# Rotary embedding on one core: four VectorE operations per batch instead of ten, and the tables in float32 on the SyncE queue

## The chip, the cores and the metric

The kernel runs on one core of one Trainium2 chip. The metric is the time of one execution in microseconds (us); medians of several runs are given, with their range. A profile gives the *span*, from the first to the last instruction of the core; here a run's time is 1.7 to 2.2 us longer than its span.

The core has several engines that work at the same time. VectorE (DVE in the profile) does all the arithmetic here, ScalarE (ACT) the small casts and the negation of the changed kernel, GpSimd (POOL) only issues transfers and SyncE (SP) issues the table transfers of the changed kernel. Sixteen DMA engines move the bytes. In the packet records (below) a transfer of a batch is 128 packets, and they start in rounds of 16; I read this as eight packets for each engine, worked off in order.

## The reference

```python
def setup_inputs():
    batch, seq_len, num_heads, head_dim = (8, 2048, 16, 64)
    return {'x': np.random.randn(batch, seq_len, num_heads, head_dim).astype(np.float32),
            'cos': np.random.randn(seq_len, head_dim // 2).astype(np.float32),
            'sin': np.random.randn(seq_len, head_dim // 2).astype(np.float32)}

def reference(x, cos, sin):
    head_dim = x.shape[-1]
    x1 = x[..., :head_dim // 2]
    x2 = x[..., head_dim // 2:]
    cos = cos[None, :, None, :]
    sin = sin[None, :, None, :]
    out1 = x1 * cos - x2 * sin
    out2 = x1 * sin + x2 * cos
    return np.concatenate([out1, out2], axis=-1).astype(np.float32)
```

The input x and the output are 8 batches of 8.39 MB each in float32 (2048 x 16 x 64 x 4 bytes). Each table has 0.26 MB.

## The kernel before

A batch is one tile of 128 partitions with 16384 float16 values each. GpSimd's queue casts from float32 on the way in and back on the way out. Five tiles can be in use. VectorE works in place, on half a batch at a time.

```python
    const_pool = ctx.enter_context(tc.tile_pool(name="rope_const", bufs=1))
    io_pool = ctx.enter_context(tc.tile_pool(name="rope_io", bufs=5))
    tmp_pool = ctx.enter_context(tc.tile_pool(name="rope_tmp", bufs=2))
    # ... load(b): one transfer on nc.gpsimd, x[b] -> a [P, J, H, D] float16 tile
    def tables():
        nc.gpsimd.dma_start(out=sin_sb, in_=sin.rearrange("(p j) d -> p (j d)", j=J))
        nc.gpsimd.dma_start(out=cos_sb, in_=cos.rearrange("(p j) d -> p (j d)", j=J))

    def rotate(xt):
        for j0 in range(0, J, JC):          # J = 16, JC = 8: two halves
            # ... v1, v2: temporaries; x1, x2: halves of the head; sin_b, cos_b: broadcasts
            nc.vector.tensor_mul(out=v1, in0=x2, in1=sin_b)      # L55
            nc.vector.tensor_mul(out=v2, in0=x1, in1=sin_b)      # L56
            nc.vector.tensor_mul(out=xw, in0=xw, in1=cos_b)      # L58
            nc.vector.tensor_sub(out=x1, in0=x1, in1=v1)         # L59
            nc.vector.tensor_add(out=x2, in0=x2, in1=v2)         # L60

    for b in range(B):
        tiles[b] = load(b)                                       # L37
        if b == 0:
            tables()                                             # L43, L44
        if b >= 4:
            nc.gpsimd.dma_start(out=out[b - 4]..., in_=tiles[b - 4])   # L68
        rotate(tiles[b])
    # ... the stores of the last four batches                     L73
```

The scheduler may reorder the instructions of one queue where the data allow it. In what follows L0 to L7 are the loads of the batches and S0 to S7 their stores.

## Time and profile before

| | before |
|---|---|
| time, median of 3 (range) | 318.91 us (318.77 to 319.09) |
| span of the profiled run | 317.2 us |
| HBM bytes | 67.63 MB read, 67.11 MB written |
| VectorE busy | 210.7 us, 66% |
| first VectorE operation | 24.26 us |
| last store issued | 265.27 us |

From the page of the kernel before: busy time, the span in 40 slices (a digit is the busy share of a slice in tenths), the DMA queue and the HBM bytes.

```profile
DVE 210.7 (66%) x80; POOL 9.9 (3%) x22
...
DVE  0009999999999999999069999995009994000000
...
DMA  7979999999999999999999999999999999999996
...
q0 software_dynamic: 2592, 100.93, 99.6%
...
HBM read 67.63 MB, written 67.11 MB: 425 GB/s over the span
```

The DMA row is the one to look at: 9 nearly from end to end. VectorE has holes. The transfers move 134.7 MB in 317.2 us, and while the row stays like this only fewer bytes or a higher rate would shorten them. The 425 GB/s is what the Trainium skill gives for a core that streams alone ("HBM Reference", Specifications (TRN2)), and near the 435 GB/s that it names as the fabric's ceiling ("DMA: Bandwidth & Descriptors", Specifications). The page puts that ceiling at the ports of the on-chip memory, where here only the float16 bytes pass, half as many.

Two of the groups of instructions (busy us, mean ns of one; then the idle time before them and what ended most of it), and the view of waits (us in total, times, longest):

```profile
L55 DVE TENSOR_TENSOR v<-xt,sin_sb 128x4096 f16<-128x4096 f16 x16 | 36.5, 2284 | 54.2 <-DMA xt<-in_x_dram 29.9
L58 DVE TENSOR_TENSOR xt<-xt,cos_sb 128x8192 f16<-128x8192 f16 x16 | 70.7, 4416 | 0.0
```

```profile
POOL xt L37 <- DMA out_dram<-xt: 118.1, 3, 56.4
...
DVE v L55 <- DMA xt<-in_x_dram: 29.9, 2, 20.2
DVE v L55 <- DMA sin_sb<-in_sin_dram: 24.3, 1, 24.3
```

GpSimd waits 118 us for stores to land before it may load a tile again. Whether that hurts is told by the order of its issues. The timeline of the kernel before (start, duration, what; in brackets the idle time before and what ended it):

```profile
2.96 2.14 POOL L37 DMA_DIRECT2D xt<-in_x_dram  x4
24.26 2.29 DVE L55 TENSOR_TENSOR v<-xt,sin_sb 128x4096 f16<-128x4096 f16 x1 [24.26 <-DMA sin_sb<-in_sin_dram]
...
53.13 0.54 POOL L68 DMA_DIRECT2D out_dram<-xt  x1 [48.03 <-DVE xt L60]
...
79.41 0.54 POOL L68 DMA_DIRECT2D out_dram<-xt  x1 [25.74 <-DVE xt L60]
...
123.00 0.54 POOL L37 DMA_DIRECT2D xt<-in_x_dram  x1 [43.05 <-DMA out_dram<-xt]
...
142.13 0.53 POOL L37 DMA_DIRECT2D xt<-in_x_dram  x1 [18.60 <-DMA out_dram<-xt]
...
142.66 1.06 POOL L68 DMA_DIRECT2D out_dram<-xt  x2
...
200.15 0.54 POOL L37 DMA_DIRECT2D xt<-in_x_dram  x1 [56.42 <-DMA out_dram<-xt]
200.67 1.05 POOL L73 DMA_DIRECT2D out_dram<-xt  x2
...
265.27 0.53 POOL L73 DMA_DIRECT2D out_dram<-xt  x1 [46.18 <-DVE xt L60]
```

Read as letters this is L0 to L4, S0 S1, L5 L6, S2 S3, L7, S4 S5 S6 S7. When L5 waits for S0 to land, S1 is already queued behind it; when L6 waits for S1, L5 is. So the engines never run dry, and GpSimd's waits cost nothing.

### The profile page before, as it was taken

To read this page: it belongs to the slowest core of one execution; us is meant where nothing else is said; L and a number is where in the kernel's file an instruction comes from. 1 tells how busy PE (TensorE), PEld (TensorE's weight loads), DVE (VectorE), ACT (ScalarE), POOL (GpSimd) and SP (SyncE) were. 2 spreads that over 40 slices of the span, in tenths; PEclk is the share of its full clock that TensorE was granted. 3 is DMA by queue.
4 is the path that set the end of the run, shared out by engine and by line. 5 is a ranking of instruction groups with operands and counts; after the bars stand their busy time and mean duration, and the time that the engine had idled before them with its cause. 6 is when DMAs were issued, how large, how long until landed. Compare 5 with 4: busy or idle time off the path is not lost.

```text
span 317.2 us, 164 instructions
## 1 busy us (share of the span) xinstructions
DVE 210.7 (66%) x80; POOL 9.9 (3%) x22
## 2 busy tenths in 40 slices
DVE  0009999999999999999069999995009994000000
POOL 5000000000000000001000000100000000000000
DMA  7979999999999999999999999999999999999996
GB/s 132 256 163 266 207 198 202 260 198 198 198 264 264 397 397 529 397 331 231 231 198 199 380 413 397 454 471 264 198 314 413 397 446 479 397 397 512 413 397 264
DMA packets 2593, 100.93 MB, mean 318 GB/s; under 512 B 288, under 2 KB 544, under 8 KB 544
## 3 DMA queue, kind: packets, MB, share of 16 engines
q0 software_dynamic: 2592, 100.93, 99.6%
q14 instruction: 1, 0.01, 0.0%
HBM read 67.63 MB, written 67.11 MB: 425 GB/s over the span
## 4 chain that ended last, share of the span: by engine, by line
issue 34%; DMA 19%; DVE 16%; another core or an unknown queue 13%; POOL 1%; POOLq 0%; DVEq 0%; PEldq 0%
DMA xt<-in_x_dram 12%; DMA sin_sb<-in_sin_dram 7%; DVE xt L58 5%; DVE v L55 3%; DVE xt L60 3%; DVE v L56 3%; DVE xt L59 2%; POOL xt L37 1%; POOL out_dram L68 1%; POOLq L101 0%; POOLq L37 0%; POOLq L73 0%; DVEq L55 0%; PEldq L101 0%
## 5 line engine op out<-in xcount | busy, mean ns | idle before, releaser
L55 DVE TENSOR_TENSOR v<-xt,sin_sb 128x4096 f16<-128x4096 f16 x16 | 36.5, 2284 | 54.2 <-DMA xt<-in_x_dram 29.9
L58 DVE TENSOR_TENSOR xt<-xt,cos_sb 128x8192 f16<-128x8192 f16 x16 | 70.7, 4416 | 0.0
L59 DVE TENSOR_TENSOR xt<-xt,v 128x4096 f16<-128x4096 f16 x16 | 36.5, 2283 | 0.1
L60 DVE TENSOR_TENSOR xt<-xt,v 128x4096 f16<-128x4096 f16 x16 | 36.5, 2283 | 0.0
L56 DVE TENSOR_TENSOR v<-xt,sin_sb 128x4096 f16<-128x4096 f16 x16 | 36.5, 2283 | 0.0
L37 POOL DMA_DIRECT2D xt<-in_x_dram x8 | 4.4, 568 | 118.9 <-DMA out_dram<-xt 118.1
L68 POOL DMA_DIRECT2D out_dram<-xt x4 | 2.1, 539 | 73.8 <-DVE xt L60 73.8
L73 POOL DMA_DIRECT2D out_dram<-xt x4 | 2.1, 532 | 63.0 <-DVE xt L60 63.0
L44 POOL DMA_DIRECT2D cos_sb<-in_cos_dram x1 | 0.5, 548 | 0.0
L43 POOL DMA_DIRECT2D sin_sb<-in_sin_dram x1 | 0.5, 542 | 0.0
L90 POOL MEMSET const-float32-0.0<- 128x1 f32 x1 | 0.1, 100 | 0.2 <-issue 0.2
L90 POOL MEMSET const-bfloat16-1.0<- 128x1 bf16 x1 | 0.1, 103 | 0.0
L90 POOL MEMSET const-float32-1.0<- 128x1 f32 x1 | 0.1, 100 | 0.0
L90 POOL MEMSET const-uint8-127<- 128x1 uint8 x1 | 0.1, 100 | 0.0
## 6 DMA issues: line engine op xcount, KB each, us to landing
xt<-in_x_dram POOLq DMA_DIRECT2D x8, 4096.0 KB, 39.8
sin_sb<-in_sin_dram POOLq DMA_DIRECT2D x1, 128.0 KB, 22.2
cos_sb<-in_cos_dram POOLq DMA_DIRECT2D x1, 128.0 KB, 22.4
out_dram<-xt POOLq DMA_DIRECT2D x8, 65.9
```

The source lines that it names most:

```text
L37: nc.gpsimd.dma_start(out=xt, in_=x[b].rearrange("(p j) h d -> p (j h d)", j=J))
L43: nc.gpsimd.dma_start(out=sin_sb, in_=sin.rearrange("(p j) d -> p (j d)", j=J))
L44: nc.gpsimd.dma_start(out=cos_sb, in_=cos.rearrange("(p j) d -> p (j d)", j=J))
L55: nc.vector.tensor_mul(out=v1, in0=x2, in1=sin_b)
L56: nc.vector.tensor_mul(out=v2, in0=x1, in1=sin_b)
L58: nc.vector.tensor_mul(out=xw, in0=xw, in1=cos_b)
L59: nc.vector.tensor_sub(out=x1, in0=x1, in1=v1)
L60: nc.vector.tensor_add(out=x2, in0=x2, in1=v2)
L68: nc.gpsimd.dma_start(out=out[b - 4].rearrange("(p j) h d -> p (j h d)", j=J), in_=tiles[b - 4])
L73: nc.gpsimd.dma_start(out=out[b].rearrange("(p j) h d -> p (j h d)", j=J), in_=tiles[b])
L90: nc = _bacc.Bacc("TRN2", target_bir_lowering=False, num_devices=1)
```

## The change

The intent is fewer, longer VectorE operations, a subtract turned into an add by a negated sine table, and tables that no longer stand in the software queue.

```diff
-    JC = 8
+    NBUF = 5
-    tmp_pool = ctx.enter_context(tc.tile_pool(name="rope_tmp", bufs=2))
+    tmp_pool = ctx.enter_context(tc.tile_pool(name="rope_tmp", bufs=1))
-    cos_sb = const_pool.tile([P, J, Dh], f16)
-    sin_sb = const_pool.tile([P, J, Dh], f16)
+    # sin_f, cos_f: float32 tiles; cos_h, sin_h, neg_h: float16 tiles
+    nc.sync.dma_start(out=sin_f, in_=sin.rearrange("(p j) d -> p j d", j=J))
+    nc.sync.dma_start(out=cos_f, in_=cos.rearrange("(p j) d -> p j d", j=J))
     # ... load unchanged; the tables() of before is gone
     def rotate(xt):
-        for j0 in range(0, J, JC):
-            # ... the five operations of a half
+        v = tmp_pool.tile([P, J, H, D], f16)
+        # ... sin_b, neg_b, cos_b: broadcasts over the heads
+        nc.vector.tensor_mul(out=v[:, :, :, 0:Dh], in0=xt[:, :, :, Dh:D], in1=neg_b)   # L58
+        nc.vector.tensor_mul(out=v[:, :, :, Dh:D], in0=xt[:, :, :, 0:Dh], in1=sin_b)   # L59
+        xw = xt.rearrange("p j h (e d) -> p j (h e) d", d=Dh)
+        nc.vector.tensor_mul(out=xw, in0=xw, in1=cos_b)                                # L61
+        xa = xt.rearrange("p j h d -> p (j h d)")
+        nc.vector.tensor_add(out=xa, in0=xa, in1=v.rearrange("p j h d -> p (j h d)"))  # L63
+    tiles = [load(b) for b in range(NBUF)]
+    nc.scalar.copy(out=sin_h, in_=sin_f)
+    nc.scalar.mul(out=neg_h, in_=sin_f, mul=-1.0)
+    nc.scalar.copy(out=cos_h, in_=cos_f)
     for b in range(B):
-        # ... load, store of b - 4, rotate
+        rotate(tiles[b])
+        store(b, tiles[b])                       # the same transfer, now L49
+        if b + NBUF < B:
+            tiles.append(load(b + NBUF))         # L43
```

More of the change, by code (lines that the diff above doesn't have):

```diff
@@ L20 @@
     f16 = mybir.dt.float16
+    f32 = mybir.dt.float32
     B, S, H, D = x.shape
@@ L25 @@
     J = S // P
-    JC = 8
+    NBUF = 5
     const_pool = ctx.enter_context(tc.tile_pool(name="rope_const", bufs=1))
-    io_pool = ctx.enter_context(tc.tile_pool(name="rope_io", bufs=5))
-    tmp_pool = ctx.enter_context(tc.tile_pool(name="rope_tmp", bufs=2))
-    cos_sb = const_pool.tile([P, J, Dh], f16)
-    sin_sb = const_pool.tile([P, J, Dh], f16)
+    io_pool = ctx.enter_context(tc.tile_pool(name="rope_io", bufs=NBUF))
+    tmp_pool = ctx.enter_context(tc.tile_pool(name="rope_tmp", bufs=1))
+    sin_f = const_pool.tile([P, J, Dh], f32)
+    cos_f = const_pool.tile([P, J, Dh], f32)
+    cos_h = const_pool.tile([P, J, Dh], f16)
+    sin_h = const_pool.tile([P, J, Dh], f16)
+    neg_h = const_pool.tile([P, J, Dh], f16)
+    nc.sync.dma_start(out=sin_f, in_=sin.rearrange("(p j) d -> p j d", j=J))
+    nc.sync.dma_start(out=cos_f, in_=cos.rearrange("(p j) d -> p j d", j=J))
     def load(b):
@@ L40, in load, with store @@
         return xt
-    def tables():
-        nc.gpsimd.dma_start(out=sin_sb, in_=sin.rearrange("(p j) d -> p (j d)", j=J))
-        nc.gpsimd.dma_start(out=cos_sb, in_=cos.rearrange("(p j) d -> p (j d)", j=J))
+    def store(b, xt):
+        nc.gpsimd.dma_start(
+            out=out[b].rearrange("(p j) h d -> p (j h d)", j=J), in_=xt
+        )
     def rotate(xt):
-        for j0 in range(0, J, JC):
-            js = slice(j0, j0 + JC)
-            v1 = tmp_pool.tile([P, JC, H, Dh], f16)
-            v2 = tmp_pool.tile([P, JC, H, Dh], f16)
-            x1 = xt[:, js, :, 0:Dh]
-            x2 = xt[:, js, :, Dh:D]
-            sin_b = sin_sb[:, js, :].unsqueeze(2).to_broadcast([P, JC, H, Dh])
-            cos_b = cos_sb[:, js, :].unsqueeze(2).to_broadcast([P, JC, 2 * H, Dh])
-            nc.vector.tensor_mul(out=v1, in0=x2, in1=sin_b)
-            nc.vector.tensor_mul(out=v2, in0=x1, in1=sin_b)
-            xw = xt[:, js, :, :].rearrange("p j h (e d) -> p j (h e) d", d=Dh)
-            nc.vector.tensor_mul(out=xw, in0=xw, in1=cos_b)
-            nc.vector.tensor_sub(out=x1, in0=x1, in1=v1)
-            nc.vector.tensor_add(out=x2, in0=x2, in1=v2)
@@ L62 @@
-    tiles = {}
-    for b in range(B):
-        tiles[b] = load(b)
-        if b == 0:
-            tables()
-        if b >= 4:
-            nc.gpsimd.dma_start(
-                out=out[b - 4].rearrange("(p j) h d -> p (j h d)", j=J), in_=tiles[b - 4]
-            )
+        v = tmp_pool.tile([P, J, H, D], f16)
+        sin_b = sin_h.unsqueeze(2).to_broadcast([P, J, H, Dh])
+        neg_b = neg_h.unsqueeze(2).to_broadcast([P, J, H, Dh])
+        cos_b = cos_h.unsqueeze(2).to_broadcast([P, J, 2 * H, Dh])
@@ L71 @@
+    nc.scalar.mul(out=neg_h, in_=sin_f, mul=-1.0)
+    nc.scalar.copy(out=cos_h, in_=cos_f)
+    for b in range(B):
         rotate(tiles[b])
-    for b in range(B - 4, B):
-        nc.gpsimd.dma_start(
-            out=out[b].rearrange("(p j) h d -> p (j h d)", j=J), in_=tiles[b]
-        )
+        store(b, tiles[b])
+        if b + NBUF < B:
+            tiles.append(load(b + NBUF))
 _INS = ['x', 'cos', 'sin']
```

## The prediction

> **What bounds the kernel now.** The transfers. In the slice table the DMA row is at 9 tenths nearly throughout; the queue table gives 99.6% of the 16 engines' span to one software queue. The kernel reads 67.63 MB and writes 67.11 MB of HBM, 425 GB/s over the 317.2 us span: 16 big transfers (8 loads, 8 stores) of 8.4 MB of float32, about 315/16 = 19.7 us each. The table by windows agrees: the load-only stretch 26 to 98 us moves 216 to 221 GB/s counted in float16, so 432 to 442 in float32; two stores back to back (98 to 142 us) move 405. VectorE is busy 210.7 us (66%), behind the transfers; it waits 29.9 us for loads of x and 24.3 us for the first data (view of waits). GpSimd's waits (118.1 us for stores to land before a buffer is loaded again) cost nothing: in the timeline other transfers are queued during each.
>
> **What the change does.** VectorE: a batch takes 8 operations of 4096 columns (start to start 2.20 us) and 2 of 8192 (4.34 us): 26.3 us. Afterwards two of 8192 and two of 16384: the same elements. The durations 2283 and 4416 ns give 0.52 ns an element, the two elements a cycle that the Trainium skill ("VectorE: DVE Perf Modes", Side-by-side) gives tensor_tensor at best; bigger operations gain no mode. Estimate: 2 x 4.34 + 2 x 8.6 = 25.9 us a batch; busy time falls from 210.7 to about 208 us, none of it critical.
>
> Tables: the first VectorE operation waited until 24.2 us for the sine table, queued behind the first load. It should start near 22 us, when the load lands. Nothing is gained at the end: the same bytes go through the same 16 engines, as the Trainium skill says ("DMA: Bandwidth & Descriptors", Issuing engines are not separate DMA queues).
>
> **Critical path.** Bytes of x and out: unchanged. Gain 0 to 1 us.
>
> **The risk: order on GpSimd's queue.** Before, the issues came as five loads, S0 S1 L5 L6 S2 S3 L7 S4 to S7 (S store, L load), so a transfer was always queued while a load waited for a store. The diff can't show the scheduled order. If it becomes S0 L5 S1 L6 S2 L7, each of the three loads waits with an empty queue. One such gap, estimated from the trace's end (312 to 317.2 us at a 0.48 share: 2.7 us lost) and start (1.9 us before any bytes), costs 3 to 4 us, so 9 to 12 us. Chance: about one in four.
>
> **Prediction.** 318.5 us; 316 to 327 holds it 8 times in 10. Faster by over 2%: 0.03. Within 2%: 0.75. Slower by over 2%: 0.22.
>
> **What would show each step right or wrong.** VectorE's groups: 8192 near 4.4 us, 16384 near 8.7 us, busy 206 to 209 us. First VectorE operation at 21 to 23 us, released by the load of x, not a table. DMA at 9 tenths in all slices; HBM bytes 0.3 MB more at most. A DMA slice at 8 or less in the middle, just after a load's wait for a store, would show the bad order.
>
> **What would make it wrong.** That order; loads and stores mixed on the engines at another rate than 405 to 440 GB/s; operations of 16384 columns at a different rate; a last load landing so late that VectorE's 26 us for it empties the queue before the last store.

## The result, and the profile after

The changed kernel took 318.04 us (median of 6, 317.98 to 318.18) and the kernel before 319.03 us (median of 6, 318.77 to 319.15) on the same chip. The difference is 1.0 us in the medians and 0.9 us in the spans of the profiled runs (316.3 against 317.2). The ratio is 0.997, with a 95% interval of 0.9957 to 0.9983. A ratio is the mean time of one kernel's fast runs over that of the other's fast runs of the same rounds, so it is not quite the ratio of the medians. Whether even this 0.3% is a property of the kernel is taken up below: on another chip it was not there.

From the page of the changed kernel, the same lines as of the kernel before:

```profile
DVE 209.2 (66%) x32; ACT 2.9 (1%) x4; POOL 8.8 (3%) x20
...
DVE  0009999999999999999579999990009993000000
...
DMA  8999999999999999999999999999999999999996
...
q0 software_dynamic: 2304, 100.66, 99.4%
q1 hardware_dynamic: 288, 0.52, 0.4%
...
HBM read 67.63 MB, written 67.11 MB: 426 GB/s over the span
```

VectorE went from 80 instructions to 32 and from 210.7 to 209.2 us. The DMA row is what it was, except for two slices: the first, where the tables arrive on queue q1, rose from 7 to 8 tenths, and the third from 7 to 9, because there L1 now follows L0 at once where the tables had stood between them. The groups and the waits:

```profile
L58 DVE TENSOR_TENSOR v<-xt,neg_h 128x8192 f16<-128x8192 f16 x8 | 35.4, 4426 | 54.1 <-DMA xt<-in_x_dram 53.9
L61 DVE TENSOR_TENSOR xt<-xt,cos_h 128x16384 f16<-128x16384 f16 x8 | 69.5, 8692 | 0.3
```

```profile
POOL xt L43 <- DMA out_dram<-xt: 120.2, 3, 56.4
DVE v L58 <- DMA xt<-in_x_dram: 53.9, 3, 24.8
```

An operation of 16384 columns takes 8.69 us and one of 8192 takes 4.42 us; before, one of 8192 took 4.42 us as well. VectorE's waits for data stay at 54 us: 29.9 for loads and 24.3 for the sine table before, 53.9 for loads now. The timeline of the changed kernel shows the same order of transfers:

```profile
1.25 2.79 POOL L43 DMA_DIRECT2D xt<-in_x_dram  x5 [0.80 <-PEq L99]
...
23.60 4.43 DVE L58 TENSOR_TENSOR v<-xt,neg_h 128x8192 f16<-128x8192 f16 x1 [23.60 <-DMA xt<-in_x_dram]
...
50.18 0.54 POOL L49 DMA_DIRECT2D out_dram<-xt  x1 [46.15 <-DVE xt L63]
...
76.43 0.54 POOL L49 DMA_DIRECT2D out_dram<-xt  x1 [25.70 <-DVE xt L63]
...
121.98 0.53 POOL L43 DMA_DIRECT2D xt<-in_x_dram  x1 [45.02 <-DMA out_dram<-xt]
...
141.29 0.53 POOL L43 DMA_DIRECT2D xt<-in_x_dram  x1 [18.78 <-DMA out_dram<-xt]
141.81 1.06 POOL L49 DMA_DIRECT2D out_dram<-xt  x2
...
199.26 0.53 POOL L43 DMA_DIRECT2D xt<-in_x_dram  x1 [56.38 <-DMA out_dram<-xt]
199.78 1.05 POOL L49 DMA_DIRECT2D out_dram<-xt  x2
...
264.13 0.53 POOL L49 DMA_DIRECT2D out_dram<-xt  x1 [50.50 <-DVE xt L63]
```

S0 goes out 3 us earlier than before (50.18 against 53.13), and S1 likewise (76.43 against 79.41), because VectorE starts 0.7 us earlier and no longer weaves two batches into each other. But L5, which waits for S0 to *land*, starts only 1 us earlier (121.98 against 123.00): S0 stands in line behind L0 to L4, and the line moves at the engines' pace.

### The profile page after: what moved, and what is told of

Same layout as the page of the kernel before. It is cut to its first block, busy times and chain, and to the rows that moved or that the text cites. A ratio compares the mean times of both kernels' runs of the same rounds, so it can differ in the third digit from the quotient of the medians.

```text
span 316.3 us, 121 instructions
## 1 busy us (share of the span) xinstructions
DVE 209.2 (66%) x32; ACT 2.9 (1%) x4; POOL 8.8 (3%) x20
## 4 chain that ended last, share of the span: by engine, by line
issue 33%; DMA 19%; DVE 17%; another core or an unknown queue 14%; POOL 1%; POOLq 0%; DVEq 0%; PEldq 0%
DMA xt<-in_x_dram 19%; DVE xt L63 6%; DVE xt L61 6%; DVE v L58 3%; DVE v L59 3%; POOL out_dram L49 1%; POOL xt L43 0%; POOLq L99 0%; POOLq L49 0%; DVEq L61 0%; DVEq L58 0%; PEldq L99 0%
## 5 line engine op out<-in xcount | busy, mean ns | idle before, releaser
L58 DVE TENSOR_TENSOR v<-xt,neg_h 128x8192 f16<-128x8192 f16 x8 | 35.4, 4426 | 54.1 <-DMA xt<-in_x_dram 53.9
L61 DVE TENSOR_TENSOR xt<-xt,cos_h 128x16384 f16<-128x16384 f16 x8 | 69.5, 8692 | 0.3
L63 DVE TENSOR_TENSOR xt<-xt,v 128x16384 f16<-128x16384 f16 x8 | 69.5, 8692 | 0.3
L59 DVE TENSOR_TENSOR v<-xt,sin_h 128x8192 f16<-128x8192 f16 x8 | 35.3, 4418 | 0.0
```

The costliest lines, as they stand in the source:

```text
L58: nc.vector.tensor_mul(out=v[:, :, :, 0:Dh], in0=xt[:, :, :, Dh:D], in1=neg_b)
L59: nc.vector.tensor_mul(out=v[:, :, :, Dh:D], in0=xt[:, :, :, 0:Dh], in1=sin_b)
L63: nc.vector.tensor_add(out=xa, in0=xa, in1=v.rearrange("p j h d -> p (j h d)"))
```

## The experiments

Eleven kernels ran. The trace also holds a record of each packet that a DMA engine moved. A load packet of x fills one partition: 65,536 bytes of float32 read, 32,768 of float16 written. A store packet is the reverse. The quickest load packets took 2.431 us and the store packets 2.447 us on average; so an engine needs 8 packets, about 19.3 us from one transfer's start to the next one's, for its share of a batch either way. (8.39 MB in 19.33 us is 434 GB/s.)

### Is VectorE anywhere in the chain? Less of it, and more of it

The first edit leaves one operation per batch of the four. The result is wrong.

```diff
-        nc.vector.tensor_mul(out=v[:, :, :, 0:Dh], ...)
-        nc.vector.tensor_mul(out=v[:, :, :, Dh:D], ...)
         nc.vector.tensor_mul(out=xw, in0=xw, in1=cos_b)
-        nc.vector.tensor_add(out=xa, ...)
```

> The changed kernel with one VectorE operation per batch (the cosine product of 16384 columns) instead of four, wrong on purpose. Theory D (the transfers alone set the time): VectorE busy falls from 209 to about 70 us and the time stays at 318.0 us within 0.3. Rival (VectorE's time sits in the chain, through the first operations or the last store): a fall of the order of the 17.4 us that one batch loses, to about 300 us.

It took 318.29 us (median of 4, 317.71 to 318.80; ratio to the kernel before 0.9978). From its page:

```profile
DVE 69.5 (22%) x8; ACT 3.0 (1%) x4; POOL 8.8 (3%) x20
...
DVE  0009155090550900000073280000009100000000
...
DMA  8999999999999999999999999999999999999996
```

VectorE lost 140 of its 209 us and the time did not follow. The rival falls.

The second edit adds a fifth operation, whose result is overwritten. The output stays right.

```diff
+        nc.vector.tensor_mul(out=v.rearrange("p j h d -> p (j h d)"), in0=x0, in1=x0)
         nc.vector.tensor_mul(out=v[:, :, :, 0:Dh], in0=xt[:, :, :, Dh:D], in1=neg_b)
```

> The changed kernel with a fifth VectorE operation of 16384 columns per batch, whose result is overwritten, so the output stays right. VectorE needs 8 x 8.7 = 70 us more. Theory D with a limit: VectorE hides until the last store goes out later than the engines run dry, near 295 us; with 34.9 us a batch from 23.6 us on it goes out near 303 us, so the time is 326 to 329 us, about 10 us more and not 70. Rival D2 (VectorE hides at any length up to the span): 318.0 us. Rival V (VectorE is on the chain throughout): 388 us.

It took 328.64 us (median of 4, 328.05 to 330.38; ratio 1.0312), as expected of VectorE with a limit. Its page, a line of its timeline and a stretch of its table by windows (start to end, length, VectorE, ScalarE and GpSimd busy, PE clock, DMA share, GB/s):

```profile
DVE 278.7 (85%) x40; ACT 2.9 (1%) x4; POOL 8.8 (3%) x20
...
DMA  8989989989989999989989999998899999990896
```

```profile
303.89 0.53 POOL L49 DMA_DIRECT2D out_dram<-xt  x1 [34.44 <-DVE xt L65]
```

```profile
295.00:304.00 9.00, 8.60 (x1) 0.00 (x0) 0.10 (x1) 1.00 0.00 0
```

The 0 near the end of the DMA row is the limit: VectorE finished the last batch at 303.6 us, and in the window from 295 to 304 us no packet begins. In the changed kernel the last store is issued at 264.1 us, and its first packet starts at 294.7 us by the packet records. VectorE thus has some 30 us of slack. Of the 70 us more work another 30 went into its own waits for loads (53.9 us in the changed kernel; here the view of waits has the line below), and only about 10 came out as time. What the change saves on VectorE (1.5 us of busy time) only makes this slack longer.

```profile
DVE v L59 <- DMA xt<-in_x_dram: 23.7, 1, 23.7
```

### Which half of the change moved the 0.3%?

One kernel has the tables alone, the other the operations alone.

```diff
 # tables alone: the kernel before, with
-        nc.gpsimd.dma_start(out=sin_sb, ...)     # and cos_sb, software queue
+    nc.sync.dma_start(out=sin_f, ...)            # and cos_f, float32, SyncE queue
+        nc.scalar.copy(out=sin_sb, in_=sin_f)    # and cos_sb
```

```diff
 # operations alone: the changed kernel, with
-    nc.sync.dma_start(out=sin_f, ...)            # and cos_f
+        nc.gpsimd.dma_start(out=sin_h, ...)      # and cos_h, after load(0)
+        nc.scalar.mul(out=neg_h, in_=sin_h, mul=-1.0)
```

> The kernel before with only the tables changed: float32 on the SyncE queue, cast by two ScalarE copies; its ten VectorE operations per batch stay. Theory T (the 0.9 us that the change gained are the tables leaving the software queue and filling the idle start): about 318.0 us, as the changed kernel, with the last packet ending 0.9 us earlier than before. Rival V (the gain comes from the four longer VectorE operations, each store going out a little earlier): 319.0 us, as before.

> The changed kernel with only its VectorE side: four operations per batch and a negated table, but the tables come as float16 on the software queue behind the first load, as before. Theory T: 319.0 us, as before. Rival V: 318.0 us.

The operations alone took 318.80 us (median of 5, 318.64 to 319.12; ratio 0.9996): as before, so nothing of the 0.3% shows on the VectorE side. The tables alone took 318.54 us (median of 6) but spread from 317.91 to 320.35 us; its ratio, 0.9996 with an interval of 0.9976 to 1.0016, decides nothing. So both it and the changed kernel ran again, side by side on another chip.

> The tables-alone kernel once more, unchanged, because its timed runs spread from 317.9 to 320.4 us and settled nothing. Theory T: median 318.0 to 318.5 us, and equal to the changed kernel run beside it. Rival V: 319.0 us, 0.9 us above the changed kernel run beside it.

> The changed kernel, unchanged, beside the two others on one chip. If its 0.9 us gain is real, its median lies 0.5 to 1.2 us under the kernel before; if not, it is within 0.3 us of it.

The tables alone took 318.94 us (median of 6, 318.54 to 320.68; ratio 1.0011). The changed kernel took 319.61 us (median of 6, 317.88 to 320.08; ratio 1.0012, interval 0.9993 to 1.0031), beside 318.98 us for the kernel before. By its own expectation the gain of 0.9 us is not confirmed; a median 0.6 us above the kernel before lies outside both outcomes. The tables alone fit neither as a whole: 318.9 us is rival V's number, but 0.7 us under the changed kernel beside it and not 0.9 above. What is there is a wider spread: with the tables on SyncE's queue runs at this speed lie between 317.7 and 320.7 us, while the kernel before stays within 318.6 to 319.3 us on every chip, the operations alone within 318.6 to 319.1 and the kernel without tables (below) within 317.3 to 317.9.

The packet records of the profiled runs show where the spread comes from. The columns: when the first and the last of the 16 engines begin with x, when they begin with S0, when the last two of them end, and the mean of all 16 ends. (The records do not name the engine; the 16 earliest packets are taken for the 16 engines' first ones, and a late engine is followed by its lateness.)

| profiled run (us) | span | begin x, first / last | begin S0, first / last | last two ends | mean end |
|---|---|---|---|---|---|
| before | 317.2 | 2.61 / 3.83 | 102.27 / 102.75 | 315.24, 315.41 | 314.98 |
| operations alone | 317.4 | 2.63 / 3.45 | 102.31 / 103.01 | 315.31, 315.50 | 315.05 |
| changed | 316.3 | 3.42 / 3.82 | 101.56 / 102.01 | 314.39, 314.50 | 314.22 |
| changed, again | 318.3 | 3.44 / 5.30 | 101.37 / 103.76 | 314.32, 316.55 | 314.26 |
| tables alone | 316.3 | 3.50 / 3.86 | 101.40 / 101.78 | 314.26, 314.59 | 314.11 |
| tables alone, again | 317.2 | 3.24 / 4.62 | 101.14 / 103.02 | 315.42, 315.50 | 314.37 |

In the profile of the repeated run the changed kernel has one engine that begins with x at 5.30 us, 1.5 us after the second latest of 3.80, and the last end stands 2.2 us after the second last. The other fifteen end by 314.32 us, 1.1 us before the last one of the kernel before. A spread at the start can shrink during the loads (in the kernel before from 1.2 us to 0.5 us by S0), but from S0 on lateness is not made up (in the repeated run the last engine is 1.9 us behind the next at S0 and 2.2 us at the end), and the slowest engine sets the time. So in all four profiles with the tables on SyncE's queue the engines end 0.6 to 0.9 us earlier on average than in the two without, the repeated ones included; and in two of the four late engines give that back or more. That the late start comes from the table packets is likely, since it was seen only with them (also in the profile of the forced order below, with two engines at 5.29 and 5.55 us), but it is not proven. On the first chip none of the changed kernel's six runs shows it, on the other most seem to; whether the chip decides, and which engine it is, stays open.

### Are the tables free on their own queue?

The tables are left out; constants stand in, and the result is wrong.

```diff
-    nc.sync.dma_start(out=sin_f, ...)            # and cos_f
-    nc.scalar.copy(out=sin_h, in_=sin_f)         # and neg_h, cos_h
+    nc.vector.memset(sin_h, 0.5)                 # and neg_h, cos_h
```

> The changed kernel with no tables loaded at all; constants are written in their place, so the result is wrong on purpose. Theory T1 (in the changed kernel the tables still cost engine time: they hold back the first packet of x from 2.6 to 3.4 us): the first packet of x starts at 2.6 us and the time is 317.2 us, 0.8 less than the changed kernel. Rival T2 (on the hardware queue the tables are free, all hidden before x starts): 318.0 us, as the changed kernel.

It took 317.58 us (median of 5, 317.31 to 317.87; ratio 0.9958), between the two expectations. The packet records decide. The first packet of x starts at 2.61 us, as T1 said. The start of L1 alone would mislead: with all engines starting at once from idle, the first round of 16 packets took 3.15 us on average instead of 2.43, and L1 began at 22.6 us. In the changed kernel x begins 0.8 us later, at 3.42 us, its first round took only 2.49 us, and L1 began at 22.8 us. In the kernel before, with 1.56 us of table packets per engine between L0 and L1 (256 packets of 98 ns over 16 engines) and a slow first round of 3.12 us, L1 began at 24.0 us. By that mark the tables on SyncE's queue would cost 0.2 us. But the four loads that follow even the slow first round out: averaged over the 16 engines, x begins at 2.87 us without tables and at 3.56 us in the changed kernel, S0 at 101.03 and 101.73 us, and the last packet ends at 313.52 and 314.22 us, 0.7 us apart each time. In the kernel before S0 begins at 102.45 us and the mean end is 314.98 us. The tables thus cost some 1.4 us on the software queue and 0.7 us on SyncE's in these profiles, late engines aside: theory T1, with 0.7 where it said 0.8. They cost less on SyncE's queue because their first packet starts at 2.01 us, 0.6 us before x could begin, and so fills idle time: 256 packets of 87 ns are 1.4 us for each engine, of which some 0.8 us are left.

The one-operation run above also shows what happens when a table packet comes too late. In its records four table packets, which I take to be one engine's, stand alone at 6.25, 8.75, 11.26 and 13.76 us, 2.5 us apart: one for each packet of x. This is what the Trainium skill says of the queues of one engine ("DMA: Bandwidth & Descriptors", Queues, rings and completion order): it takes turns between them, a whole packet at a time. A 2,048-byte table packet beside 65,536-byte packets waits for a whole one of them each time.

### The order that the prediction feared

Each store is tied, in issue order only, behind the transfer that precedes it in the source.

```diff
     def store(b, xt):
+        with tc.issue_after(queued[-1].ins):
             queued.append(nc.gpsimd.dma_start(out=out[b]..., in_=xt))
```

> The changed kernel with its transfers forced into the order in which the source writes them: five loads, S0 L5 S1 L6 S2 L7 S3 to S7. Theory Q (my prediction's risk: loads 5, 6 and 7 each wait for a store with nothing else queued): three gaps in the DMA row near 120, 160 and 200 us of 3 to 4 us each, so 327 to 330 us. Rival (the engines do not all finish together, the fast ones work on while the slow ones end, and the gap is smaller or hidden): 318 to 322 us.

It took 332.34 us (median of 4, 331.07 to 333.62; ratio 1.0422), 13 us more, and a little over the range that I had given. Its DMA row and queue share, and its timeline:

```profile
DMA  7989899898998939989889989789999989899995
...
q0 software_dynamic: 2304, 100.66, 96.5%
```

```profile
124.25 0.53 POOL L45 DMA_DIRECT2D xt<-in_x_dram  x1 [71.11 <-DMA out_dram<-xt]
124.77 0.54 POOL L52 DMA_DIRECT2D out_dram<-xt  x1
167.32 0.53 POOL L45 DMA_DIRECT2D xt<-in_x_dram  x1 [42.02 <-DMA out_dram<-xt]
167.85 0.54 POOL L52 DMA_DIRECT2D out_dram<-xt  x1
210.53 0.53 POOL L45 DMA_DIRECT2D xt<-in_x_dram  x1 [42.15 <-DMA out_dram<-xt]
```

L5 waits for S0 with nothing behind S0. By the packet records the engines stand idle for 4.55, 2.44 and 2.45 us on average at the three places: 9.4 us, within the 9 to 12 that the prediction estimated. The first gap is the longer because two engines, late from the start, end S0 2.2 us after the others; from the last end to the first new packet it is 1.9 us at all three places. The rest is in the packets. Of L5, L6 and L7 the first round took 3.06, 3.00 and 3.21 us and the last round, before the store, 3.78, 3.90 and 3.60 us, against 2.43 in between: about 2 us for each load, 6.0 us in all. Together 15.4 us, of the 15.6 us between the spans (331.8 and 316.3 us). The profiled run is the slowest of the four (333.62 us). With three gaps of 2.4 us and 6.0 us of slow packets, an estimate without late engines gives 13.3 us, near the 13.4 us between the medians. The first five loads, which start from idle too, have the same slow last round before the store that follows: 2.8 to 3.7 us in L4 in every profile of the table.

Is it the idling or the taking turns? The next kernel keeps the alternation but starts it one store later: S0 S1 L5 S2 L6 S3 L7 S4 to S7.

```diff
-        if b + NBUF < B:
-            tiles.append(load(b + NBUF))
+        if b >= 1 and b + NBUF - 1 < B:
+            tiles.append(load(b + NBUF - 1))
```

> The changed kernel with its transfers forced into five loads, S0 S1 L5 S2 L6 S3 L7 S4 to S7: loads and stores still take turns, but each load that waits for a store has one more store queued before it. Theory Q (what cost 13 us in the strictly alternating order was the empty queue and the restart after it): no gap in the DMA row, loads 5 to 7 with packets of 2.43 us, 318.0 us. Rival A (taking turns between a load and a store costs by itself, about 2 us a load, as the slow packets of loads 5 to 7 there would allow): about 324 us.

It took 318.40 us (median of 6, 317.74 to 319.57; ratio 0.9984). Its DMA row has no gap, and the packets of L5, L6 and L7 took 2.43 us in every round. Taking turns costs nothing that shows here; an empty queue does, by its gap and by the slow restart after it.

```profile
DMA  8999999999999999999999999999999999999996
```

### Would loads and stores overlap if they were mixed finely?

A load reads twice the bytes it writes, and a store writes twice the bytes it reads. If the two sides of an engine were limited on their own, mixing would win. L3 to L7 and all stores are cut into 16 transfers each; in the first kernel their pieces take turns, in the control they do not. In both VectorE works in quarters of a batch and only three loads stand ahead.

```diff
+                for j in range(J):
+                    load_cut(b + AHEAD, j)       # AHEAD = 3
+                    store_cut(b, j)              # control: all load cuts, then all store cuts
```

> The changed kernel with loads 3 to 7 and all stores cut into 16 transfers of 0.5 MB of float32 each, and load and store pieces put in turn on the software queue. Theory F (a descriptor takes the time of its float32 side, 65536 bytes in 2.43 us, whatever stands next to it): no gain from the mixing, 318 us plus a cost for smaller descriptors, 320 to 335 us, equal to the run with the same cut and no mixing. Rival M (a load is limited by its reads and a store by its writes, so the two overlap when mixed finely): up to a quarter of the mixed 197 us goes, 270 to 300 us.

> The control of the mixed run: the same cut into 16 pieces, but all pieces of a load and then all pieces of a store. Theory F: the same as the mixed run within 1%, 320 to 335 us. Rival M: 320 to 335 us here and 20 us or more less in the mixed run.

They took 331.02 us (ratio 1.0369) and 330.90 us (ratio 1.0374), medians of 4. The mixed kernel's DMA row and rates, then the rates of the control:

```profile
DMA  8999999899999999999999999999999999999991
GB/s 191 242 195 234 207 203 242 185 318 321 308 314 322 309 310 323 315 307 320 319 307 316 322 310 311 322 314 308 320 320 307 342 420 423 420 422 421 421 421 40
...
GB/s 191 243 203 219 219 199 243 163 210 211 415 419 301 209 233 421 420 275 210 259 421 422 248 209 288 422 420 219 210 321 420 422 419 422 421 421 422 421 421 70
```

The flat 307 to 323 GB/s in the middle, where the control swings between 209 and 422, shows that the mixing did take place, and it won nothing: theory F stands. Packets of 4,096 bytes on the float32 side took 173 ns on average in the loads and 189 ns in the stores, but their records overlap; by the rate of the last stores, 421 GB/s, 16 engines moved one each in 156 ns, where a sixteenth of a 65,536-byte packet would take 152. Mixing within an engine finer than eight packets at a time was not tried.

None of the eleven kernels points to one that beats both by more than a few tenths of a per cent. At 19.33 us a transfer, 16 transfers take 309.3 us; with a first packet at 2.6 us at the earliest and 1.8 us from the last packet to the end of the span, that makes 313.7 us of the 316.3. The other 2.6 us are, to within 0.2, the later start of x (1.0), the slow rounds of the first five loads (1.5) and the wait for the slowest engine at the end (0.3).

## Why the prediction was right

- **The bound.** "The transfers" was right: without three quarters of VectorE's operations the time stays, and with a third more work on VectorE it rises by about 10 us only because the queue ran dry at the end.
- **VectorE's cost.** 8192 columns were said to take near 4.4 us and measured 4.42; 16384 were said to take near 8.7 and measured 8.69. Busy time was given as 206 to 209 us and was 209.2, just outside. The mis-sized term is the 8.6 us from start to start of two long operations: it was 8.73 (32.46 to 41.19 us). In the changed kernel the add starts only when the cosine product has ended (41.19 after 41.15 us), where before, operations could overlap (26.47 us, before the end of the first at 26.55). A batch takes VectorE 26.3 us in both kernels. The 0.52 ns an element agrees with the two a cycle of the Trainium skill's table ("VectorE: DVE Perf Modes", Side-by-side, with the 0.96 GHz given there).
- **The first operation.** It is released by the load of x and not by a table, as said. It came at 23.6 us and not at 21 to 23. The prediction took 19.7 us for the load alone; but the first packet starts only at 3.4 us, and eight packets of 2.43 us and the landing follow.
- **The end.** "Gain 0 to 1 us" held on the first chip (1.0 us in the medians) and not on another (a median 0.6 us slower). The mechanism named, that the bytes go through the same engines on either queue, is right, for the tables still cost engine time there. What "nothing is gained at the end" missed is when they run: partly before x can begin, so they cost 0.7 us instead of 1.4. That gain is in every profile on average; now and then an engine starts late and takes it back.
- **The risk of the order.** The scheduler kept the order, so the risk did not come about. Nothing in the prediction said that it would; that part was a bet at three to one that held. Its size was under-estimated when the order was forced: 13 us in time, where I had said 9 to 12. The gap itself was over-estimated, 2.4 us against 3 to 4 where the engines end together; that the profile's idle sum of 9.4 us fits is luck, since 2 us of it are the wait for the two late engines. The missing term is the slow packets of a load that starts from idle, 2.0 us for each of the three.
- **Mixing.** The prediction listed another rate for mixed loads and stores as something that could prove it wrong. There is none, in transfers that take turns or in pieces that do.

## What to carry to other kernels

When the DMA row is at 9 from end to end, count bytes, and do not expect time from fewer or longer VectorE operations; measure how much slack VectorE has (30 us here) before you spend work on it. Look at the order of issues on the queue: in this kernel, whose transfers last 19.3 us, a load that waits for a store is free as long as one other transfer stands queued behind that store, and costs some 4.4 us each time if none does (a gap of 2.4 us and 2.0 us of slow packets), and more when an engine is late. A difference of 0.3% between two kernels that both saturate the engines should be measured on more than one chip before it is called a gain.

## What the Trainium skill lacked or had wrong

- "DMA: Bandwidth & Descriptors" gives a fixed cost per transfer, but not what a restart from idle costs: a load of 4 MB in float16 after an empty queue had first packets of 3.0 to 3.2 us and last packets before a store of 3.6 to 3.9 us instead of 2.43, 2.0 us a load, on top of a gap of 2.4 us (4.6 us where two engines were late). A load that followed a store without a gap paid neither.
- The same page does not say what a casting transfer is limited by. Here a packet took 2.43 to 2.45 us for 65,536 bytes on its float32 side, whether that was the read or the write side, and mixing loads with stores did not make the two overlap (331.0 against 330.9 us).
- The same page calls a packet preferably at most 4,096 bytes (SWDGE vs HWDGE vs iDMA). The trace records packets of 65,536 bytes for contiguous rows, and an engine took turns with the other queue at that grain: table packets 2.5 us apart. Whether the trace's packets are the page's is not said there.
- The same page puts the first byte of a hardware-queue transfer at about 0.6 us and of a software one at about 1 us. Counted from the start of the issuing instruction it was longer here: 1.27 us from 0.74 to the first table packet at 2.01 in the changed kernel (1.0 us in the other profiles with this queue), and 1.36 us from 1.25 to the first packet of x at 2.61 in the kernel before. Counted from the instruction's end, at 1.11 and 1.92 us, it was 0.6 to 0.9 and 0.7 us. The page does not say where it counts from, so these runs do not show it wrong.
- None of the pages says that an engine's lateness stays with it while the queue is full: one that began S0 1.9 us after the others ended 2.2 us after them, 213 us later.
